# One inference step of a hybrid streaming encoder: a quarter of each weight tile's low half on GpSimd, gate1 summed on VectorE

## The chip, the core and the metric

The kernel runs on one core of a Trainium2 chip. The core has five engines with queues of their own: TensorE (PE; PEld is its weight load), VectorE (DVE), ScalarE (ACT), GpSimd (POOL) and SyncE (SP), which here issues most of the loads. The metric is the time of one execution on the device, in microseconds (us).

## What is computed

One layer of an encoder step, for 256 prompt tokens and 32 sample tokens with shared weights, D_MODEL = 2048:

```
sh1, sc1, g1, sh2, sc2, g2 = split(silu(c) @ w_mod + b_mod)      # w_mod 2048 x 12288, two rows of c
h = rms_norm(x) * (1 + sc1) + sh1
P = h @ w_in                                                     # 2048 x 14864
branch A: gated linear recurrence, 8 heads (chunkwise scan)
branch B: Mamba-2 SSD, 16 heads, convolution of width 4
branch C: chunked gMLP spatial gating
merged = sum_k sigmoid(g_k) * (y_k @ w_branch_k)
x = x + g1 * (merged @ w_out)
x = x + g2 * (relu(h2 @ w_up) ** 2 @ w_down)                     # h2 = rms_norm(x) * (1 + sc2) + sh2
y = rms_norm(x)
```

All data are float32; the states of both recurrences are outputs too.

## The kernel before

**Products.** TensorE multiplies in the type fp32r, so both factors are split into a high half (the value cast to fp32r) and a low half (what is left). Activations are split once (`hhi`/`hlo`, `yhi`/`ylo`, `mhi`/`mlo`, `h2hi`/`h2lo`, `uhi`/`ulo`). Weights are split as they arrive: `weights` (line 447) loads a tile of 128 x 4 x 256 floats (512 KB) with SyncE into one of 6 `raw` buffers, and `halves` (line 440) makes `whi` from it on ScalarE (line 443) and `wlo` on VectorE (line 444); there are 3 buffers of each. `product_group` (line 453) then does 24 matmuls per tile into two PSUM tiles: for each of 2 column blocks and 4 row blocks i, `whi` by the low activations, `whi` by the high ones and `wlo` by the high ones (lines 461 to 463). 512 tiles go this way; 56 more, of the first phase, go through `product_part` (line 418) and `halves` in the same manner.

**Order.** First phase: shift and scale of the first norm (parts 0 and 1 of w_mod) are multiplied while h is made and the first columns of `w_in` run. Then come branch C, the eight heads of branch A with their projections (`mixer_a`, line 672; until about 650 us), the sixteen of branch B (`mixer_b`), the branch products, `w_out` (about 1100 us), and from 1200 us on `w_up` and `w_down` in four slices. The recurrences take many small instructions of VectorE, ScalarE and TensorE, and some of GpSimd (memsets, copies into `att`, loads and stores of states).

**The other parts of w_mod.** They are fed in between: after each weight tile `product_group` moves a generator by a rate (`mod_rate`), and each step loads 512 KB of w_mod into a `raw` buffer (`mraw`). The order is part 2 (gate1, needed by `evac_out` from about 1100 us on), then 4, 3 and 5. Part 2 is multiplied on TensorE (lines 339 to 347): for each pair of row blocks a group of 16 entries in the trace, four column groups side by side, 32 columns wide, between other matmuls (`together`, lines 77 and 80). Parts 4, 3 and 5 are summed on VectorE (`mod_part_ve`, line 302): two multiply-adds of 128 x 512 for each of 2 row blocks of a step (line 318), one for each of the two rows of c. A unit of 512 columns ends in `mod_flush` (line 360): matmuls with ones sum over the partitions (line 375), ScalarE copies, a transpose turns (line 380), VectorE adds the bias (line 383).

**Order within an engine.** A scheduler lays the instructions of each engine into one fixed order, by the program's order and by priorities; loads and halves of weights carry a priority of 2500 places, evacuations of 1500. Each engine then runs its order strictly.

Of the kernel before, what the change touches and what calls it, by code (L numbers as in the profile page):

```python
# [10 lines left out]
F32 = mybir.dt.float32  # L11
# [3 lines left out]
ALU = mybir.AluOpType  # L15
PSUM = bass.MemoryType.PSUM

P = 128
D = 2048
NB = D // P  # L20
# [20 lines left out]
def tile_step(ctx, tc, io, outs):  # L41
    nc = tc.nc
# [8 lines left out]
    PRIO = 2500  # L51

    MOD_PARTS = (2, 4, 3, 5)
    MOD_VE = (4, 3, 5)


    MODR, RS, RA, RB, RD, RW, RC = 1.5, 0.2, 0.4, 0.3, 0.5, 0.5, 0.25

    RAW, WHI, WLO = 6, 3, 3
    MTAG = ("raw", RAW)  # L60

    MODB = 2
    EVB = 6
    BLK = 34
    TMPB = 10
# [5 lines left out]
    def nm(s):  # L71
        uid[0] += 1
        return f"{s}_{uid[0]}"

    def together(works):

        first = works[0]()  # L77
        with tc.issue_after(first.ins), tc.high_priority(offset=PRIO):
            for work in works[1:]:
                work()  # L80
# [96 lines left out]
    with tc.high_priority(offset=2 * PRIO):  # L177
        ps = aux()
# [78 lines left out]
    def par(name, j, n=1):  # L257
        i, r = off[name]
        return pcols[i][:, r + j:r + j + n]
# [42 lines left out]
    def mod_part_ve(part):  # L302


        for u in range(4):
            c0 = part * D + u * 512
            acc = [wpool.tile([P, 512], F32, tag="macc", name=nm("macc"), bufs=2) for _ in range(2)]
            for q in range(8):
                with tc.high_priority(offset=PRIO):
                    raw = wpool.tile([P, 2, 512], F32, tag=MTAG[0], name=nm("mraw"), bufs=MTAG[1])  # L310
                    nc.sync.dma_start(out=raw, in_=wm[:, 2 * q:2 * q + 2, c0:c0 + 512])
                for i in range(2):
                    for s in range(2):
                        cs = cT[:, 2 * q + i, s:s + 1]
                        if q == 0 and i == 0:
                            V.tensor_scalar_mul(out=acc[s], in0=raw[:, i], scalar1=cs)
                        else:
                            V.scalar_tensor_tensor(out=acc[s], in0=raw[:, i], scalar=cs, in1=acc[s],  # L318
                                                   op0=ALU.mult, op1=ALU.add)
                if q == 1:  # L320
                    mod_flush()
                yield
            ps = paux.tile([P, 512], F32, tag="modps", name=nm("modps"), bufs=2)
            mod_tail.append((part * NB + u * 4, 0, ps, acc))
        mod_flush()

    def mod_parts(parts):


        for part in parts:  # L330
            if part in MOD_VE:
                yield from mod_part_ve(part)
                continue
            for half in range(2):
                ps = paux.tile([P, 512], F32, tag="modps", name=nm("modps"), bufs=2)
                c0 = part * D + half * 1024
                held = []
                for k in range(NB):
                    with tc.high_priority(offset=PRIO):
                        raw = wpool.tile([P, 1024], F32, tag=MTAG[0], name=nm("mraw"), bufs=MTAG[1])  # L340
                        nc.sync.dma_start(out=raw, in_=wm[:, k, c0:c0 + 1024])
                    held.append((k, raw))
                    if len(held) == MODB:
                        together([partial(TE.matmul, ps[32 * cg:32 * cg + 32, 0:256], cT[:, k1, :],
                                          r[:, cg * 256:(cg + 1) * 256], start=k < MODB and k1 == k,
                                          stop=k == NB - 1 and k1 == held[0][0])
                                  for k1, r in reversed(held) for cg in range(4)])
                        held = []
                    if k == 1:
                        mod_flush()  # L350
                    yield
                with tc.high_priority(offset=PRIO):
                    sb = wpool.tile([P, 256], F32, tag="modsb", name=nm("modsb"), bufs=1)
                    S.copy(out=sb, in_=ps[:, 0:256])
                mod_tail.append((part * NB + half * 8, 0, ps, sb))
        mod_flush()

    mod_tail = []

    def mod_flush():  # L360

        while mod_tail:
            j, n, ps, sb = mod_tail.pop()
            if n:
                for b in range(n):
                    TE.matmul(ps[:, 2 * b:2 * b + 2], sb[:, b * P:(b + 1) * P], selm, start=True, stop=True)
                V.tensor_tensor(out=mod[:, j:j + n, :],
                                in0=ps[:, 0:2 * n].rearrange("p (b s) -> p b s", s=2),
                                in1=par("b_mod", j, n).unsqueeze(2).to_broadcast([P, n, 2]), op=ALU.add)
            else:  # L370
                nb = 2
                if type(sb) is list:
                    nb = 1
                    acc, sb = sb, wpool.tile([P, 256], F32, tag="modsb", name=nm("modsb"), bufs=1)
                    together([partial(TE.matmul, ps[32 * cg:32 * cg + 32, 0:P], ones2[:, s],
                                      acc[s][:, cg * P:(cg + 1) * P], start=s == 0, stop=s == 1)
                              for s in range(2) for cg in range(4)])
                    S.copy(out=sb[:, 0:P], in_=ps[:, 0:P])
                for b in range(nb):
                    TE.transpose(ps[:, b * P:(b + 1) * P], sb[:, b * P:(b + 1) * P], ident)  # L380
                v = ps[:, 0:nb * P].rearrange("p (b g r) -> p g b r", b=nb, r=32)
                m = mod[:, j:j + 4 * nb, :].rearrange("p (g b) s -> p g b s", b=nb)
                V.tensor_tensor(out=m, in0=v[:, :, :, 0:2], op=ALU.add,
                                in1=par("b_mod", j, 4 * nb).rearrange("p (g b) -> p g b", b=nb).unsqueeze(3)
                                .to_broadcast([P, 4, nb, 2]))


    KG = ((0, 2), (2, 2), (4, 2), (6, 2), (8, 4), (12, 4))
    boot = [(part * D + k0 * P, nk * P) for k0, nk in KG for part in (0, 1)]
    mods = chain(mod_stream(boot), mod_parts(MOD_PARTS))  # L390

    mod_count = [0]

# [43 lines left out]
                else:  # L437
                    V.tensor_add(out=acc, in0=acc, in1=pt)

    def halves(raw):  # L440
        whi = wpool.tile(list(raw.shape), F32R, tag="whi", name=nm("whi"), bufs=WHI)
        wlo = wpool.tile(list(raw.shape), F32R, tag="wlo", name=nm("wlo"), bufs=WLO)
        S.copy(out=whi, in_=raw)  # L443
        V.tensor_sub(out=wlo, in0=raw, in1=whi)  # L444
        return whi, wlo

    def weights(wv, col, q):
        with tc.high_priority(offset=PRIO):
            raw = wpool.tile([P, 4, 256], F32, tag="raw", name=nm("raw"), bufs=RAW)
            nc.sync.dma_start(out=raw, in_=wv[:, q:q + 4, col:col + 256])  # L450
            return halves(raw)

    def product_group(wv, col, nk, ahi, alo, evac, j0, n=T):
        pts = [pmain.tile([P, n], F32, tag="mm", name=nm("mm")) for _ in range(2)]
# [881 lines left out]
```

## Time and profile before

| | |
|---|---|
| median of 3 runs | 2058.45 us (2055.4 to 2059.97) |
| the profiled execution | 2054.64 us, its span 2052.9 us |
| TensorE / VectorE / ScalarE / GpSimd busy | 2002.9 / 1450.8 / 990.9 / 154.8 us |
| granted TensorE clock, mean | 0.993 |
| DMA | 412 MB, 201 GB/s on average |

Busy times count each moment once, though instructions of an engine can overlap: the next one's record begins before the last one's ends. A wait in the trace is idle time of an engine, put down to what released it. A granted clock of 1.00 is 2.4 GHz.

### The profile page before, as it was taken

The numbers are of one execution on the slowest core, as the hardware profiler recorded it, in microseconds if no ns is written. First come the engines' busy times: TensorE is split into PE (matmuls) and PEld (weight loads), VectorE is DVE, ScalarE is ACT, GpSimd is POOL, SyncE is SP. The second block draws the span as 40 slices with busy tenths as digits, with TensorE's granted clock in tenths as the row PEclk, the third lists the DMA queues.
The fourth block names the chain that finished last, engine by engine and source line by source line (L and its number), as shares of the span: only waits on it lengthen the run. The fifth ranks groups of instructions, "written<-read, shape, count | busy, mean of one in ns | idle before, by whom it ended". The sixth has DMA issues, their size and how long they took to land.

```text
span 2052.9 us, 40220 instructions
## 1 busy us (share of the span) xinstructions
PE 2002.9 (98%) x16248; PEld 1941.6 (95%) x16248; DVE 1450.8 (71%) x2515; ACT 990.9 (48%) x1547; POOL 154.8 (8%) x284
## 2 busy tenths in 40 slices
PE   5999999999999999999999999999999999999997
PEld 3888999989999999999999999999999999999997
DVE  2585767866679878798889998675864455555564
ACT  3432595675555545555344544433443344334443
POOL 3020220100101101011000100000000000000010
PEclk8999999999999999999999999999999999999999
DMA  9998745556576766577777777575655555555542
GB/s 259 312 315 267 224 137 165 176 166 200 184 226 191 212 192 199 174 229 242 226 248 235 228 237 225 185 226 185 218 192 163 162 163 166 168 165 162 167 157 88
DMA packets 364874, 412.29 MB, mean 201 GB/s; under 512 B 14808, under 2 KB 325488, under 8 KB 364688
## 3 DMA queue, kind: packets, MB, share of 16 engines
q1 hardware_dynamic: 360784, 403.97, 63.2%
q0 software_dynamic: 3040, 4.58, 1.0%
q8 instruction: 127, 2.08, 0.4%
q10 hardware_dynamic: 864, 1.18, 0.2%
q14 instruction: 59, 0.48, 0.1%
HBM read 405.05 MB, written 4.62 MB: 200 GB/s over the span
## 4 chain that ended last, share of the span: by engine, by line
PE 61%; DVE 0%; ACT 0%; DMA 0%; issue 0%; DVEq 0%; ACTq 0%
PE mm L463 20%; PE mm L461 20%; PE mm L462 20%; DMA mraw<-in_w_mod_dram 0%; PE aux L1226 0%; PE aux L210 0%; ACT stage L1300 0%; PE aux L897 0%; PE modps L77 0%; PE modps L80 0%; PE aux L80 0%; PE aux L936 0%; DVE macc L318 0%; PE aux L885 0%; DVE wlo L444 0%
## 5 line engine op out<-in xcount | busy, mean ns | idle before, releaser
L443 ACT CAST whi<-raw 128x1024 fp32r<-128x1024 f32 x568 | 595.4, 1049 | 835.9 <-PE mm L462 652.8
L444 DVE TENSOR_TENSOR wlo<-raw,whi 128x1024 fp32r<-128x1024 f32 x568 | 695.2, 1225 | 410.5 <-ACT whi L443 408.8
L461 PE MATMUL mm<-hlo,whi 128*128 128x288 f32 x1408 | 419.8, 299 | 1.2 <-ACT sg L974 1.2
L462 PE MATMUL mm<-hhi,whi 128*128 128x288 f32 x1408 | 417.1, 297 | 0.0
L463 PE MATMUL mm<-hhi,wlo 128*128 128x288 f32 x1408 | 412.3, 297 | 1.7 <-DVE wlo L444 1.7
L461 PE MATMUL mm<-h2lo,whi 128*128 128x290 f32 x1024 | 304.4, 298 | 0.0
L462 PE MATMUL mm<-h2hi,whi 128*128 128x290 f32 x1024 | 303.7, 297 | 0.0
L463 PE MATMUL mm<-uhi,wlo 128*128 128x288 f32 x1024 | 303.2, 296 | 0.0
L463 PE MATMUL mm<-h2hi,wlo 128*128 128x290 f32 x1024 | 301.8, 297 | 0.0
L462 PE MATMUL mm<-uhi,whi 128*128 128x288 f32 x1024 | 301.3, 294 | 0.0
L461 PE MATMUL mm<-ulo,whi 128*128 128x288 f32 x1024 | 301.0, 294 | 0.0
L318 DVE SCALAR_TENSOR_TENSOR macc<-mraw,cT,macc 128x512 f32<-128x512 f32 x360 | 261.3, 754 | 29.8 <-DMA mraw<-in_w_mod_dram 29.6
L461 PEld LDWEIGHTS mm<-hlo,whi 128*128 128x128 f32 x1408 | 265.5, 189 | 4.7 <-issue 2.2
L463 PEld LDWEIGHTS mm<-hhi,wlo 128*128 128x128 f32 x1408 | 263.2, 189 | 3.7 <-DVE wlo L444 2.6
L462 PEld LDWEIGHTS mm<-hhi,whi 128*128 128x128 f32 x1408 | 265.9, 189 | 0.5
L463 PEld LDWEIGHTS mm<-h2hi,wlo 128*128 128x128 f32 x1024 | 194.3, 190 | 0.3 <-issue 0.2
L462 PEld LDWEIGHTS mm<-h2hi,whi 128*128 128x128 f32 x1024 | 194.5, 190 | 0.0
L461 PEld LDWEIGHTS mm<-h2lo,whi 128*128 128x128 f32 x1024 | 193.6, 189 | 0.5 <-issue 0.4
L461 PEld LDWEIGHTS mm<-ulo,whi 128*128 128x128 f32 x1024 | 193.0, 188 | 0.4 <-issue 0.4
L462 PEld LDWEIGHTS mm<-uhi,whi 128*128 128x128 f32 x1024 | 192.4, 188 | 0.0
L463 PEld LDWEIGHTS mm<-uhi,wlo 128*128 128x128 f32 x1024 | 192.2, 188 | 0.1
L430 PE MATMUL mm<-hlo,whi 128*128 128x288 f32 x448 | 136.8, 306 | 0.4 <-DVE hlo L530 0.4
(421 smaller groups left out, 3079.8 us busy)
## 6 DMA issues: line engine op xcount, KB each, us to landing
raw<-in_w_in_dram SPq DMA_DIRECT2D x204, 512.0 KB, 4.4
mraw<-in_w_mod_dram SPq DMA_DIRECT2D x128, 512.0 KB, 4.3
raw<-in_w_up_dram SPq DMA_DIRECT2D x128, 512.0 KB, 3.8
raw<-in_w_down_dram SPq DMA_DIRECT2D x128, 512.0 KB, 3.5
raw<-in_w_mod_dram SPq DMA_DIRECT2D x64, 512.0 KB, 5.9
raw<-in_w_branch_dram SPq DMA_DIRECT2D x48, 512.0 KB, 4.5
raw<-in_w_out_dram SPq DMA_DIRECT2D x32, 512.0 KB, 4.7
raw<-in_w_in_dram SPq DMA_DIRECT2D x56, 256.0 KB, 5.1
```

Of the source, the lines that this page charges most:

```text
L318: V.scalar_tensor_tensor(out=acc[s], in0=raw[:, i], scalar=cs, in1=acc[s], op0=ALU.mult, op1=ALU.add)
L430: TE.matmul(pt, whi[:, i, cs], alo[k], start=i == 0, stop=False)
L443: S.copy(out=whi, in_=raw)
L444: V.tensor_sub(out=wlo, in0=raw, in1=whi)
L461: TE.matmul(pts[b], whi[:, i, cs], alo[k], start=k == 0, stop=False)
L462: TE.matmul(pts[b], whi[:, i, cs], ahi[k], start=False, stop=False)
L463: TE.matmul(pts[b], wlo[:, i, cs], ahi[k], start=False, stop=k == nk - 1)
```

## The change

`halves` gets a flag. For the 512 tiles of `weights`, VectorE subtracts only the first three of the tile's four row blocks (768 of 1024 columns), and GpSimd the fourth. The 56 tiles of the first phase stay whole on VectorE. And part 2 of w_mod goes the way of the other three, `mod_part_ve`; the function for TensorE goes.

```
     def halves(raw, shared=False):
...
         S.copy(out=whi, in_=raw)
-        V.tensor_sub(out=wlo, in0=raw, in1=whi)
+        n = 3 if shared else raw.shape[1]
+        V.tensor_sub(out=wlo[:, 0:n], in0=raw[:, 0:n], in1=whi[:, 0:n])
+        if shared:
+            G.tensor_sub(out=wlo[:, 3], in0=raw[:, 3], in1=whi[:, 3])
         return whi, wlo

     def weights(wv, col, q):
...
-            return halves(raw)
+            return halves(raw, True)

-    def mod_parts(parts):
...
-                    if len(held) == MODB:
-                        together([partial(TE.matmul, ps[32 * cg:32 * cg + 32, 0:256], cT[:, k1, :],
-                                          r[:, cg * 256:(cg + 1) * 256], start=k < MODB and k1 == k,
-                                          stop=k == NB - 1 and k1 == held[0][0])
-                                  for k1, r in reversed(held) for cg in range(4)])
...
-    mods = chain(mod_stream(boot), mod_parts(MOD_PARTS))
+    mods = chain(mod_stream(boot), *[mod_part_ve(part) for part in MOD_PARTS])
```

The rest of the diff is `mod_flush`, whose branch for part 2's two tails goes; the sums and the transpose of a VectorE unit stay as they were.

The order on VectorE, before, near the 103rd low half, while a head of branch A ends (`stA` are its states, `pad` a copy for it):

```order
L444 TENSOR_TENSOR wlo_5793<-raw_5790,whi_5792 128x1024
L444 TENSOR_TENSOR wlo_5823<-raw_5820,whi_5822 128x1024
L600 COPY pad_106<-aux_5409 32x128
L444 TENSOR_TENSOR wlo_5892<-raw_5889,whi_5891 128x1024
L700 COPY stA_5421<-aux_5417 128x128
L701 SCALAR_TENSOR_TENSOR stA_5422<-stA_5421,eb_5399,aux_5417 128x128
L703 SCALAR_TENSOR_TENSOR stA_5423<-sA_5415,eb_5399,aux_5417 128x128
```

And now, at the 103rd low half (L405 is the subtract, L315 part 2's multiply-add, L663 to L666 are the states):

```order
L405 TENSOR_TENSOR wlo_5864<-raw_5861,whi_5863 128x768
L663 COPY stA_5300<-aux_5296 128x128
L315 SCALAR_TENSOR_TENSOR macc_5561<-mraw_5923,cT,macc_5561 128x512
L315 SCALAR_TENSOR_TENSOR macc_5562<-mraw_5923,cT,macc_5562 128x512
L664 SCALAR_TENSOR_TENSOR stA_5301<-stA_5300,eb_5278,aux_5296 128x128
L666 SCALAR_TENSOR_TENSOR stA_5302<-sA_5294,eb_5278,aux_5296 128x128
L315 SCALAR_TENSOR_TENSOR macc_5561<-mraw_5923,cT,macc_5561 128x512
L405 TENSOR_TENSOR wlo_5895<-raw_5892,whi_5894 128x768
L315 SCALAR_TENSOR_TENSOR macc_5562<-mraw_5923,cT,macc_5562 128x512
```

Part 2's multiply-adds, 128 in all, now lie between the subtracts from the 30th to the 138th low half; 39 of them between the 100th and the 120th.

The order on GpSimd, before, around a head of branch A (`atc` and `att` are its scores, `sA` and `stA` states that go in and out):

```order
L664 COPY att_5098<-atc_5099 32x32
L676 MEMSET atc_5272 128x96
L695 DMA sA_5415<-in_state_hgrn_dram 128x128
L705 DMA out_dram<-stA_5249 128x128
```

And now, around a head's end (L407 is the quarter):

```order
L625 COPY att_5323<-atc_5324 32x2x32 x4
L627 COPY att_5323<-atc_5324 32x32
L407 TENSOR_TENSOR wlo_6216<-raw_6213,whi_6215 128x256
L407 TENSOR_TENSOR wlo_6259<-raw_6256,whi_6258 128x256
L639 MEMSET atc_6394 128x96
L658 DMA sA_6537<-in_state_hgrn_dram 128x128
L668 DMA out_dram<-stA_5474 128x128
L669 DMA out_dram<-stA_5475 128x128
L407 TENSOR_TENSOR wlo_6290<-raw_6287,whi_6289 128x256
```

GpSimd had one queue of the recurrences' own work; now 512 quarters, each of which TensorE's matmuls of row block 3 wait for, stand between it.

## Rows read from the trace of the kernel before

**Rows 1.** The page's busy times: us, share of the span, instructions.
```profile
PE 2002.9 (98%) x16248; PEld 1941.6 (95%) x16248; DVE 1450.8 (71%) x2515; ACT 990.9 (48%) x1547; POOL 154.8 (8%) x284
```
**Rows 2.** Waits: engine, line, tile <- releaser: us in total, times, longest.
```profile
ACT whi L443 <- PE mm L462: 652.8, 364, 3.6
...
PE aux L77 <- DVE z L632: 2.9, 1, 2.9
...
PE mm L463 <- DVE wlo L444: 1.7, 2, 1.1
```
**Rows 3.** Busy us by stretch: length, PE, PEld, DVE, ACT, POOL (xcount), clock, DMA.
```profile
200.00:600.00 400.00, 391.27 (x3688) 372.21 (x3687) 285.31 (x612) 254.15 (x404) 51.46 (x98) 0.99 0.61 185
457.00:532.00 75.00, 73.82 (x797) 69.77 (x796) 47.69 (x103) 42.50 (x68) 6.91 (x17) 1.00 0.65 196
600.00:1000.00 400.00, 396.42 (x3298) 389.96 (x3298) 350.45 (x628) 219.79 (x355) 47.26 (x91) 1.00 0.68 208
1000.00:1200.00 200.00, 200.00 (x1553) 197.81 (x1552) 183.72 (x300) 88.09 (x140) 13.93 (x11) 1.00 0.75 234
1100.00:1200.00 100.00, 100.00 (x776) 98.53 (x775) 97.36 (x176) 47.73 (x85) 13.93 (x11) 1.00 0.73 228
```
**Rows 4.** Timeline of PE around one group (start, us), and all its matmuls on L80.
```profile
404.40 0.29 PE L462 MATMUL mm<-hhi,whi 128*128 128x288 f32 x1
404.54 0.29 PE L463 MATMUL mm<-hhi,wlo 128*128 128x288 f32 x1
...
405.76 0.51 PE L724 MATMUL aux<-sq,ones 128*128 128x288 f32 x1
...
L80 PE MATMUL modps<-mraw,cT x224: 379/379/404, 206.0 to 585.9; 128*32 128x256 f32 x112
```
**Rows 5.** Timeline of PE around the tail of a VectorE unit.
```profile
874.44 0.30 PE L463 MATMUL mm<-yhi,wlo 128*128 128x288 f32 x1
...
875.24 0.40 PE L461 MATMUL mm<-hlo,whi 128*128 128x288 f32 x1
```
**Rows 6.** Groups: xcount | busy us, mean ns | idle before <- releaser.
```profile
L444 DVE TENSOR_TENSOR wlo<-raw,whi 128x1024 fp32r<-128x1024 f32 x568 | 695.2, 1225 | 410.5 <-ACT whi L443 408.8
...
L318 DVE SCALAR_TENSOR_TENSOR macc<-mraw,cT,macc 128x512 f32<-128x512 f32 x360 | 261.3, 754 | 29.8 <-DMA mraw<-in_w_mod_dram 29.6
...
L1249 DVE TENSOR_TENSOR ulo<-r,uhi 128x288 fp32r<-128x288 f32 x64 | 28.7, 452 | 0.1
```
**Rows 7.** Timeline of DVE and POOL from 961 to 964 us.
```profile
961.13 0.75 DVE L318 SCALAR_TENSOR_TENSOR macc<-mraw,cT,macc 128x512 f32<-128x512 f32 x1
...
961.79 1.22 DVE L444 TENSOR_TENSOR wlo<-raw,whi 128x1024 fp32r<-128x1024 f32 x1
...
962.93 1.31 DVE L318 SCALAR_TENSOR_TENSOR macc<-mraw,cT,macc 128x512 f32<-128x512 f32 x1
...
961.94 1.74 POOL L949 TENSOR_TENSOR ssB<-ssB,sq 128x288 f32<-128x288 f32 x1 [16.63 <-ACT sq L944]
```
**Rows 8.** Timeline of POOL and DVE at 227 us.
```profile
227.22 0.82 POOL L1031 TENSOR_TENSOR sumC<-sumC,acc 128x288 f32<-128x288 f32 x1 [0.32 <-ACT acc L1026]
...
227.21 0.45 DVE L438 TENSOR_TENSOR acc<-acc,mm 128x288 f32<-128x288 f32 x1 [0.61 <-PE mm L432]
```
**Rows 9.** DVE's subtracts (L444) alone by the stretches of rows 3: length, busy (xcount).
```profile
200.00:600.00 400.00, 124.02 (x101) 0.99 0.61 185
457.00:532.00 75.00, 24.31 (x20) 1.00 0.65 196
600.00:1000.00 400.00, 136.81 (x112) 1.00 0.68 208
1000.00:1200.00 200.00, 73.08 (x60) 1.00 0.75 234
1100.00:1200.00 100.00, 35.33 (x30) 1.00 0.73 228
```
**Rows 10.** A group of DMA issues on POOL.
```profile
L202 POOL DMA_DIRECT2D xs<-in_x_sample_dram x16 | 8.8, 559 | 0.4 <-issue 0.4
```

More of the change, by code (lines that the diff above doesn't have):

```diff
@@ L53, in tile_step @@
     MOD_PARTS = (2, 4, 3, 5)
-    MOD_VE = (4, 3, 5)
     MODR, RS, RA, RB, RD, RW, RC = 1.5, 0.2, 0.4, 0.3, 0.5, 0.5, 0.25
@@ L60, in tile_step @@
     MTAG = ("raw", RAW)
-    MODB = 2
     EVB = 6
@@ L325, in mod_part_ve @@
         mod_flush()
-    def mod_parts(parts):
[L330 to L342, printed above, removed]
-                    if len(held) == MODB:
-                        together([partial(TE.matmul, ps[32 * cg:32 * cg + 32, 0:256], cT[:, k1, :],
-                                          r[:, cg * 256:(cg + 1) * 256], start=k < MODB and k1 == k,
-                                          stop=k == NB - 1 and k1 == held[0][0])
-                                  for k1, r in reversed(held) for cg in range(4)])
[L348 to L356, printed above, removed]
     mod_tail = []
@@ L370, in mod_flush @@
             else:
[L371 to L385, printed above, removed]
+                sums, sb = sb, wpool.tile([P, P], F32, tag="modsb", name=nm("modsb"), bufs=1, padded_shape=[P, 512])
+                together([partial(TE.matmul, ps[32 * cg:32 * cg + 32, 0:P], ones2[:, s],
+                                  sums[s][:, cg * P:(cg + 1) * P], start=s == 0, stop=s == 1)
+                          for s in range(2) for cg in range(4)])
+                S.copy(out=sb, in_=ps[:, 0:P])
+                TE.transpose(ps[:, 0:P], sb, ident)
+                V.tensor_tensor(out=mod[:, j:j + 4, :], in0=ps[:, 0:P].rearrange("p (g r) -> p g r", r=32)[:, :, 0:2],
+                                in1=par("b_mod", j, 4).unsqueeze(2).to_broadcast([P, 4, 2]), op=ALU.add)
     KG = ((0, 2), (2, 2), (4, 2), (6, 2), (8, 4), (12, 4))
     boot = [(part * D + k0 * P, nk * P) for k0, nk in KG for part in (0, 1)]
-    mods = chain(mod_stream(boot), mod_parts(MOD_PARTS))
+    mods = chain(mod_stream(boot), *[mod_part_ve(part) for part in MOD_PARTS])
     mod_count = [0]
@@ L438, in product_part, with halves @@
                     V.tensor_add(out=acc, in0=acc, in1=pt)
-    def halves(raw):
+    def halves(raw, shared=False):
         whi = wpool.tile(list(raw.shape), F32R, tag="whi", name=nm("whi"), bufs=WHI)
```

## The prediction

> **What bounds the kernel now.** First the page's busy times: TensorE is busy for 98% of the span, VectorE (DVE) for 71%, GpSimd (POOL) for 8% [rows 1]. Then the list of waits, because a busy share says nothing of who waits for whom: TensorE's matmuls waited for a low half (`wlo`) twice in the whole span, 1.7 us together, while ScalarE waited 364 times, 652.8 us, for TensorE to give back a buffer of high halves [rows 2]. So the weights are always ready ahead of TensorE, by up to the three buffers of `whi` and `wlo`, and a shorter DVE instruction is worth nothing by itself: only matmul work that goes away shortens the span, and only as long as nobody else becomes late. Last the busy time by stretches, for DVE's reserve: 285.3 of 400 us from 200 to 600 us, 350.5 of 400 to 1000, 183.7 of 200 to 1200, and in the last 100 us of that 97.36 while TensorE was still at 100.00 [rows 3]. The last row is the yardstick: DVE may be 97% busy and still hold nobody up.
>
> **The change part by part.**
>
> *Matmuls of part 2 (gate1) go.* In the trace one of them is a group of 16: the last matmul before it starts at 404.54, the next after it at 405.76, against 0.14 between neighbours without a group [rows 4]. That is 1.22 - 0.14 = 1.08 us, and the 224 matmuls of line 80, 14 of each group, make 16 groups between 206 and 586 us [rows 4]: 17.3 us of TensorE time. All of it lies on the path, since TensorE is the bound.
>
> *Four tails come instead of two.* A tail of the DVE kind holds TensorE from 874.44 to 875.24, 0.80 - 0.14 = 0.66 us [rows 5], and a transpose of at most 0.14 after it: 0.8 us, four times, 3.2 us; the two tails that go had two transposes each and no sums, some 0.5 us together. Net on TensorE: -17.3 + 3.2 - 0.5 = **-14.6 us**.
>
> *128 multiply-adds come to DVE.* They are the kind that takes 754 ns on average [rows 6]; back to back one starts 0.66 us after the other (961.13 and 961.79) [rows 7]. In the new order they stand between the 30th and the 138th low half, so nearly all in the stretch from 200 to 600 us: 120 x 0.66 = 79 us there. 39 of them stand between the 100th and the 120th low half, which were made from 457 to 532 us.
>
> *DVE's subtract shrinks to 768 columns.* 1024 columns take 1225 ns, 288 take 452 [rows 6]: 1.05 ns a column, so 768 take 0.96 us and each tile saves 0.27 us. 512 of the 568 tiles are shared (138 us over the span). ScalarE's cast and the loads stay as they are; part 2's 32 loads of 512 KB stay 32 loads of the same size, in rows half as long.
>
> *The quarter goes to POOL.* No row has a 128x256 subtract there. A 128x288 addition takes 0.82 us beside a DVE instruction that reads PSUM [rows 8], so the quarter is between 0.73 (by its columns) and 0.82 us. 512 of them are 400 us of an engine with 1900 us free, beside TensorE's 3.2 us per tile.
>
> *What the quarter does to DVE.* This is the open price. At 961.94 POOL's addition of two SBUF tiles waits behind DVE's subtract (until 963.01) and ends 0.67 us after it; the DVE multiply-add that follows takes 1.31 us, not 0.75 [rows 7]. So DVE lost 0.56 us to one POOL instruction of 288 columns, 0.50 for 256. Where the next DVE instruction takes an operand from PSUM it lost nothing: 0.45 us at 227.21, as without POOL [rows 8]. The Trainium skill says it as a rule ("SBUF — State Buffer", section "Who interferes with whom"): a DVE instruction with two SBUF inputs and a GpSimd instruction that reads SBUF exclude each other, and the later one blocks fully until the first is done. The trace agrees, with 0.56 us lost where the rule at its worst would take the whole 0.82; by that worst the change comes out as rival C at its upper end.
>
> Per tile DVE therefore changes by -0.27 us (POOL never in the way) up to -0.27 + 0.56 = +0.29 us (always). By the order about 65% of DVE's instructions read two SBUF tiles; 0.65 x 0.50 - 0.27 = **+0.06 us**, which I take: the quarter does not relieve DVE at all, it roughly pays for itself.
>
> *Is DVE still below its limit?* From 200 to 600 us 82 of the 101 tiles [rows 9] are shared: 285.3 + 79 + 82 x 0.06 = 369 us, with bounds 342 and 388, in a stretch that now lasts 400 - 14.6 = 385 us. That is 96%, just under the yardstick. The tight place is 457 to 532 us: 47.7 [rows 3] + 39 x 0.66 + 20 x 0.06 = 74.6 us (bounds 68 and 79) in 72 us (75 without its share, a fifth, of the groups that go). The two tiles, 6 us, that lie ready ahead of TensorE could hide the overhang of 2.6 us, but it will not come evenly: I count 3 us (bounds 0 and 8). From 1100 to 1200 us there are 97.4 + 30 x 0.06 = 99 us (89 to 106) of 100: 1 us (0 to 6). From 600 to 1000 even the upper bound is 350.5 + 112 x 0.29 = 383 of 400.
>
> *Waits for the recurrences.* TensorE runs in order and waited once 2.9 us for a DVE product of the A mixer [rows 2]. With DVE fuller these products come later, but the new order also puts their matmuls later, by up to 200 of the main matmuls. I take +3 us (bounds -5 and +8).
>
> *POOL's queue.* It runs in order, and behind memsets, state transfers and copies into `att` the next quarter waits. A DMA issue holds POOL 0.56 us [rows 10]. The usual bunch is three of them and a memset, 2 us, less than the lead of two tiles; the longest, ten issues (5.6 us) near 965 us, about equals it. 0 us (up to 3).
>
> **The sum.** -14.6 + 3 + 1 + 3 = -7.6 us. The profiled execution took 2054.64 us, of it 2052.9 in the span: 2047.0. It lies 3.8 us below the median of the runs shown (2058.45, from 2055.4 to 2059.97), so the forecast in terms of that median is **2051 us**, -0.4%. A measurement of this kernel can tell 0.2% (4 us) from no change.
>
> **The rivals.**
> - *A, the forecast* (0.35): DVE stays just under full, TensorE keeps half of what it won; 2045 to 2053.
> - *D, all of it* (0.15): POOL finds gaps or runs beside DVE instructions that read PSUM; DVE is relieved by up to 0.27 us per tile, nobody is late, and the later place of the A mixer's matmuls saves a few of the old waits. -14.6 - 3: 2041. For it: DVE sat idle 408.8 us before its subtracts, waiting for ScalarE's cast [rows 6], so there are gaps; against it that most of them lie after 1200 us, where DVE is not needed.
> - *B, nothing to see* (0.18): the overhang of the tight places adds up to 10 to 15 us at the bounds above, or POOL's queue holds a quarter up now and then; 2055 to 2062. That is also the case in which the change does not do what it says: DVE has as much to do as before.
> - *C, slower* (0.32): one mechanism, DVE blocked behind the quarter, on two sides of its limit. Its place is every shared tile up to 1200 us. It decides once a quarter costs DVE more than 0.53 us on average: then 82 x 0.26 = 21 us fill the stretch to 600 us (364 without any such cost, of 385). At a block of 0.67 us on every tile (net +0.40) DVE needs 397 of 385 us there, 208 of 200 from 1000 to 1200, and with the tight places' 15: +12 + 8 + 7 - 14.6, about 2071 in terms of the median. At the whole 0.82 (net +0.55) it needs 409 of 385, 412 of 400 and 217 of 200: +24 + 12 + 17 - 14.6 = +38, 2097. For it speaks that `raw` and `whi` are two SBUF tiles on both engines and that both are released by the same cast; against it that the measured loss was 0.56 and often nothing.
>
> **How the numbers follow.** The likeliest case gives 2051 us; its own range is 2045 to 2053. The range of 8 in 10 reaches from D with its waits saved, 2037, into the lower half of C, 2083; above it about 0.15 is left out, below it 0.03. Faster by over 0.2% are A and D, 0.50; within 0.2% is B, 0.18; slower is C, 0.32.
>
> **What would show it.** Right: TensorE's instructions lose the 128 wide `modps<-mraw` matmuls and its busy time falls by 13 to 16 us; DVE's multiply-adds rise from 360 to 480 with a mean above 754 ns, and its busy time rises by about 120 us (bounds -45 and 240); the subtract of 768 columns has a mean well above 0.96 us, and POOL's quarter one above 0.82, because they block each other; TensorE's waits for `wlo` stay below 10 us. D: the 768-column subtract at 0.96 us. C: DVE at 97% or more from 200 to 600 and from 600 to 1200 us, TensorE waiting for `wlo` (DVE's three quarters or POOL's one) for tens of us, and a granted clock below 0.99 there. The forecast is wrong if TensorE's busy time does not fall, or if POOL's queue rather than DVE is what it waits for.

## The result and the profile after

The change makes the kernel **slower: 2123.82 us** (median of 4 runs, 2121.04 to 2125.63) against 2059.21 us (2055.4 to 2062.64; one run more than in the table ahead), a ratio of 1.031 [1.030, 1.033]. The forecast was 2051 us, 2037 to 2083, faster. The direction was wrong, and the time lies beyond the upper end of the range.

The page's busy times of the changed kernel, to be held against [rows 1]:

```profile
PE 2014.6 (95%) x16056; PEld 1952.1 (92%) x16056; DVE 1512.1 (71%) x2645; ACT 1009.5 (48%) x1561; POOL 787.8 (37%) x796
```

TensorE (PE) has 192 instructions fewer: the 256 entries of part 2's wide matmuls are gone, as foreseen, and 64 of the tails' sums came. Yet it is 11.7 us busier, and it stands idle for 2123.9 - 2014.6 = 109.3 us instead of 50.0. VectorE (DVE) is 71% busy, as before. Of the waits (engine, line, tile <- releaser: us in total, times, longest) these matter; in the numbering of this kernel L403 is ScalarE's cast, L405 DVE's three quarters, L407 POOL's quarter, L424 to L426 are the matmuls, and L413 is the issue of a weight tile's load on SyncE:

```profile
PE mm L426 <- DVE wlo L405: 24.6, 27, 3.2
...
PE aux L74 <- DVE mpad L892: 9.4, 4, 5.7
...
PE mm L424 <- ACT whi L403: 6.7, 2, 4.9
PE aux L1027 <- DVE yC L1032: 5.4, 2, 3.8
...
ACT whi L403 <- PE mm L425: 456.5, 234, 5.8
ACT whi L403 <- POOL wlo L407: 72.8, 39, 2.5
...
SPq L413 <- POOL wlo L407: 135.6, 233, 1.1
```

Where TensorE waited twice for a low half [rows 2], it now waits 27 times (and twice in the first phase, 1.3 us), and each time for DVE: nowhere in the list of its waits is POOL's quarter. Over the whole list, TensorE's waits that DVE ended come to 55.1 us, against 8.7 before: 25.9 for low halves (1.7 before) and 29.2 for DVE's other products, above all of the recurrences and of branch C (7.0 before). Those that ScalarE ended rose from 11.9 to 22.4. ScalarE's cast, which before waited for TensorE to give a buffer back and for loads, now also waits 39 times until POOL gives a buffer of high halves back, and the loads wait 233 times until POOL gives back `raw`. The stretches (length, PE, PEld, DVE, ACT, POOL busy, clock, DMA), beside [rows 3]:

```profile
200.00:600.00 400.00, 367.25 (x3304) 353.97 (x3303) 347.44 (x705) 237.12 (x381) 126.44 (x163) 0.96 0.57 173
457.00:532.00 75.00, 70.01 (x663) 67.30 (x663) 73.68 (x149) 40.75 (x64) 24.48 (x38) 0.98 0.66 195
600.00:1000.00 400.00, 373.08 (x3047) 361.83 (x3045) 319.72 (x582) 224.89 (x349) 151.27 (x192) 0.99 0.62 186
1000.00:1200.00 200.00, 199.31 (x1549) 196.71 (x1548) 185.53 (x278) 89.45 (x131) 78.36 (x75) 1.00 0.76 235
1200.00:1600.00 400.00, 391.42 (x2943) 387.41 (x2943) 303.49 (x455) 171.49 (x267) 159.53 (x128) 1.00 0.65 206
```

From 200 to 600 us DVE is 87% busy and TensorE idle for 33 us; from 600 to 1000 us DVE is *less* busy than before (320 against 350 of 400) and TensorE idle for 27 us. So DVE does not run out of time on the whole; single instructions come late. The time is lost in pieces of at most 5.7 us from 200 to 1450 us, and nothing after that (TensorE idle for 10.9 us, before 11.1).

The groups (xcount | busy us, mean ns | idle before), beside [rows 6]:

```profile
L407 POOL TENSOR_TENSOR wlo<-raw,whi 128x256 fp32r<-128x256 f32 x512 | 650.9, 1272 | 1004.3 <-ACT whi L403 961.3 <-PE mm L425 7.3 <-DVE sg L944 4.5
L405 DVE TENSOR_TENSOR wlo<-raw,whi 128x768 fp32r<-128x768 f32 x512 | 506.6, 993 | 341.7 <-ACT whi L403 337.5 <-PE aux L687 2.9
L315 DVE SCALAR_TENSOR_TENSOR macc<-mraw,cT,macc 128x512 f32<-128x512 f32 x480 | 392.2, 852 | 61.5 <-DMA mraw<-in_w_mod_dram 60.6
```

DVE's subtract takes 0.99 us, near the 0.96 of the estimate; the quarter takes 1.27 us, not 0.73 to 0.82, and the multiply-adds 852 ns, not 754. The timelines of DVE and of POOL show how that comes:

```profile
622.69 0.95 DVE L405 TENSOR_TENSOR wlo<-raw,whi 128x768 fp32r<-128x768 f32 x1
623.56 1.88 DVE L315 SCALAR_TENSOR_TENSOR macc<-mraw,cT,macc 128x512 f32<-128x512 f32 x2
...
622.70 1.53 POOL L407 TENSOR_TENSOR wlo<-raw,whi 128x256 fp32r<-128x256 f32 x1 [1.27 <-ACT whi L403]
```

Both begin when the cast is done, DVE runs first, POOL ends 0.59 us after it, and the two multiply-adds behind take 1.88 us where two back to back take 0.66 + 0.75 = 1.41 [rows 7]. It is the mutual block of [rows 7] again; below it is called the lock. So it goes for 253 of the 512 quarters: they start together with DVE's subtract and end between 0.59 and 0.60 us after it (the middle eight tenths of them).

One long stall, of ScalarE and then of TensorE (timelines of the changed kernel):

```profile
968.34 0.42 ACT L889 ACTIVATE m<-m 128x256 f32<-128x256 f32 x1 [3.26 <-DVE m L886]
968.78 1.28 ACT L937 ACT_TABLE_LOAD   x1
970.07 0.41 ACT L937 ACTIVATE sg<-mm 128x288 f32<-128x288 f32 x1
970.50 1.28 ACT L888 ACT_TABLE_LOAD   x1
...
973.04 1.28 ACT L937 ACT_TABLE_LOAD   x1
974.34 0.41 ACT L937 ACTIVATE sg<-mm 128x288 f32<-128x288 f32 x1
974.76 1.28 ACT L889 ACT_TABLE_LOAD   x1
...
976.82 0.25 ACT L891 ACTIVATE mpad<-mpad 32x64 f32<-32x64 f32 x1
...
971.53 0.29 PE L424 MATMUL mm<-ylo,whi 128*128 128x288 f32 x1
977.47 0.29 PE L74 MATMUL aux<-mpad,xdt 128*64 128x32 f32 x1 [5.65 <-DVE mpad L892]
...
981.92 0.44 PE L425 MATMUL mm<-hhi,whi 128*128 128x288 f32 x1
982.16 0.43 PE L426 MATMUL mm<-hhi,wlo 128*128 128x288 f32 x1
...
982.95 0.30 PE L425 MATMUL mm<-hhi,whi 128*128 128x288 f32 x1
983.08 0.29 PE L426 MATMUL mm<-hhi,wlo 128*128 128x288 f32 x1
```

In the new order two gates (`sg`, sigmoid) stand between the exponentials of a head of branch B. Each change between the two makes ScalarE load a table, 1.28 us; `mpad` comes late and TensorE waits 5.65 us. And that is not all: its clock was granted at half for a stretch that begins in the stall, as the windows say (columns as above):

```profile
960.00:971.00 11.00, 10.83 (x82) 10.61 (x81) 7.45 (x14) 5.61 (x9) 3.49 (x5) 1.00 0.72 226
...
975.61:982.43 6.82, 4.96 (x28) 4.66 (x29) 4.87 (x10) 3.16 (x6) 1.50 (x1) 0.50 0.48 139
```

At 1.2 GHz matmuls start 0.24 us apart (981.92, 982.16), at 2.4 GHz 0.13 (982.95, 983.08).

Over the span the mean granted clock fell from 0.993 to 0.984. By the clock in the trace, TensorE was busy at half the clock for 46.8 us, before for 14.2; half of such time is lost, so this costs 23.4 - 7.1 = 16.3 us. With 59.3 us more idle time and the 14.6 us that went, this makes +61 of the 71 us between the two profiled spans; the other 10 lie in a busy time that I can't split further.

### The profile page after: what moved, and what is told of

Same layout as the page of the kernel before. It is cut to its first block, busy times and chain, and to the rows that moved or that the text cites. A ratio compares the mean times of both kernels' runs of the same rounds, so it can differ in the third digit from the quotient of the medians.

```text
span 2123.9 us, 41480 instructions
## 1 busy us (share of the span) xinstructions
PE 2014.6 (95%) x16056; PEld 1952.1 (92%) x16056; DVE 1512.1 (71%) x2645; ACT 1009.5 (48%) x1561; POOL 787.8 (37%) x796
## 5 line engine op out<-in xcount | busy, mean ns | idle before, releaser
L407 POOL TENSOR_TENSOR wlo<-raw,whi 128x256 fp32r<-128x256 f32 x512 | 650.9, 1272 | 1004.3 <-ACT whi L403 961.3
L403 ACT CAST whi<-raw 128x1024 fp32r<-128x1024 f32 x568 | 594.4, 1048 | 783.9 <-PE mm L425 456.5
L405 DVE TENSOR_TENSOR wlo<-raw,whi 128x768 fp32r<-128x768 f32 (+1 forms) x568 | 576.0, 1017 | 389.8 <-ACT whi L403 385.4
L315 DVE SCALAR_TENSOR_TENSOR macc<-mraw,cT,macc 128x512 f32<-128x512 f32 x480 | 392.2, 852 | 61.5 <-DMA mraw<-in_w_mod_dram 60.6
L426 PE MATMUL mm<-hhi,wlo 128*128 128x288 f32 x1408 | 421.5, 303 | 14.3 <-DVE wlo L405 14.1
L424 PE MATMUL mm<-hlo,whi 128*128 128x288 f32 x1408 | 424.0, 302 | 7.6 <-ACT whi L403 6.7
L425 PE MATMUL mm<-hhi,whi 128*128 128x288 f32 x1408 | 423.0, 301 | 0.0
L426 PE MATMUL mm<-uhi,wlo 128*128 128x288 f32 x1024 | 304.0, 297 | 2.3 <-DVE wlo L405 2.3
L424 PE MATMUL mm<-h2lo,whi 128*128 128x290 f32 x1024 | 305.6, 298 | 0.0
L426 PE MATMUL mm<-h2hi,wlo 128*128 128x290 f32 x1024 | 304.0, 297 | 0.0
L424 PE MATMUL mm<-ulo,whi 128*128 128x288 f32 x1024 | 302.8, 296 | 0.0
L426 PEld LDWEIGHTS mm<-hhi,wlo 128*128 128x128 f32 x1408 | 269.1, 192 | 19.1 <-DVE wlo L405 18.1
L424 PEld LDWEIGHTS mm<-hlo,whi 128*128 128x128 f32 x1408 | 270.5, 192 | 9.9 <-ACT whi L403 7.2
L425 PEld LDWEIGHTS mm<-hhi,whi 128*128 128x128 f32 x1408 | 270.8, 192 | 0.4
L426 PEld LDWEIGHTS mm<-uhi,wlo 128*128 128x128 f32 x1024 | 193.1, 189 | 2.8 <-DVE wlo L405 2.8
L426 PEld LDWEIGHTS mm<-h2hi,wlo 128*128 128x128 f32 x1024 | 195.4, 191 | 0.2 <-DVE wlo L405 0.2
L424 PEld LDWEIGHTS mm<-ulo,whi 128*128 128x128 f32 x1024 | 193.9, 189 | 0.5 <-issue 0.4
L424 PEld LDWEIGHTS mm<-h2lo,whi 128*128 128x128 f32 x1024 | 193.8, 189 | 0.3 <-issue 0.2
```

The costliest lines, as they stand in the source:

```text
L405: V.tensor_sub(out=wlo[:, 0:n], in0=raw[:, 0:n], in1=whi[:, 0:n])
L407: G.tensor_sub(out=wlo[:, 3], in0=raw[:, 3], in1=whi[:, 3])
L424: TE.matmul(pts[b], whi[:, i, cs], alo[k], start=k == 0, stop=False)
L425: TE.matmul(pts[b], whi[:, i, cs], ahi[k], start=False, stop=False)
L426: TE.matmul(pts[b], wlo[:, i, cs], ahi[k], start=False, stop=k == nk - 1)
```

## The experiments

All times in us; "idle" is the profiled span less TensorE's busy time; "tables" are ScalarE's table loads. Each ratio is to the kernel before as timed beside that run (medians 2057.7 for runs 1 to 4, 2059.2 for 5 to 8, 2059.8 for 9 to 11, 2059.6 for 12). Busy time, idle time and clock are those of one profiled execution; the mean clock of executions of one kernel differs by up to 0.006 (0.985 to 0.991 in run 3), so smaller differences in that column say nothing.

| kernel | median | ratio to before | PE busy | idle | clock | tables |
|---|---|---|---|---|---|---|
| before (with the change) | 2059.2 | | 2002.9 | 50.0 | 0.993 | 82 |
| the change | 2123.8 | 1.031 | 2014.6 | 109.3 | 0.984 | 94 |
| 1 part 2 alone | 2065.8 | 1.0038 [1.0023, 1.0053] | 1998.3 | 66.4 | 0.988 | 91 |
| 2 quarter alone | 2103.7 | 1.0222 [1.0206, 1.0238] | 2020.7 | 82.4 | 0.988 | 94 |
| 3 quarter as memsets | 2072.0 | 1.0066 [1.0043, 1.0090] | 2000.7 | 73.8 | 0.985 | 94 |
| 4 quarter of a constant | 2104.1 | 1.0222 [1.0198, 1.0247] | 2012.8 | 90.1 | 0.983 | 94 |
| 5 before, no tables | 2046.7 | 0.9936 [0.9918, 0.9955] | 1998.4 | 46.7 | 0.994 | 6 |
| 6 the change, no tables | 2091.4 | 1.0154 [1.0135, 1.0172] | 2003.3 | 86.3 | 0.989 | 6 |
| 7 part 2, no tables | 2049.5 | 0.9951 [0.9934, 0.9968] | 1990.0 | 55.4 | 0.991 | 6 |
| 8 memsets, no tables | 2047.1 | 0.9938 [0.9918, 0.9958] | 1989.9 | 57.0 | 0.996 | 6 |
| 9 part 2 spread | 2055.9 | 0.9979 [0.9970, 0.9988] | 1993.6 | 61.2 | 0.995 | 82 |
| 10 half of part 2, no tables | 2039.8 | 0.9902 [0.9887, 0.9917] | 1990.6 | 48.7 | 0.992 | 6 |
| 11 constant, no tables | 2076.4 | 1.0079 [1.0065, 1.0093] | 2003.5 | 71.5 | 0.987 | 6 |
| 12 part 2 spread more | 2047.3 | 0.9949 [0.9934, 0.9964] | 1989.1 | 56.8 | 0.992 | 76 |

### 1. Part 2 alone

To the kernel before:

```
-    MOD_VE = (4, 3, 5)
+    MOD_VE = (2, 4, 3, 5)
```

> The kernel before with part 2 summed on DVE and no quarter on GpSimd. Four theories stand for the +65 us of the change. Lock: a quarter on POOL and a two-SBUF instruction of DVE hold each other up, so both come late. Hold: POOL returns raw and whi late (ScalarE's cast waited 72.8 us for POOL in the changed kernel), lock or not. Part 2: the 128 multiply-adds fill DVE from 200 to 600 us, the quarter is harmless. Order: the new order of ScalarE and DVE (94 table loads on ScalarE instead of 82) is what makes the recurrences late. Lock and Hold expect 2045 to 2057 us (TensorE loses 14.6 us, the tight place from 457 to 532 us takes up to 10 back), with no wait of ScalarE's cast for POOL. Part 2 expects 2095 to 2125. Order expects something between, 2060 to 2100, since the order here is new too.

Measured: 2065.8 us, +8. Only the interval of the order theory holds that. TensorE's waits and ScalarE's timeline in this kernel (L443 is the cast, L461 the matmul that needs it):

```profile
PE mm L461 <- ACT whi L443: 7.3, 5, 4.9
```

```profile
283.31 1.28 ACT L813 ACT_TABLE_LOAD   x1
284.60 0.44 ACT L813 ACTIVATE ldt<-ldt 16x288 f32<-16x288 f32 x1
285.06 1.28 ACT L814 ACT_TABLE_LOAD   x1
286.35 0.44 ACT L814 ACTIVATE ldt<-ldt 16x288 f32<-16x288 f32 x1
286.70 1.03 ACT L443 CAST whi<-raw 128x1024 fp32r<-128x1024 f32 x1
```

The wait of 4.9 us is for the cast at 286.70, which stands behind table loads. So even without POOL TensorE did not keep its 14.6 us: it is 16.4 us more idle, and in this execution another 6.9 us go to the half clock while it works (14.0 against 7.1).

### 2. The quarter alone

To the kernel before: the new `halves` and its call, with part 2 left on TensorE.

> The kernel before with the quarter on GpSimd alone; part 2 stays on TensorE. Lock and Hold expect most of the loss without the 14.6 us won: 2100 to 2140 us, with the cast waiting tens of us for POOL and TensorE idle some 50 us or more between 200 and 1450 us. Part 2 expects 2055 to 2065, as before. Order expects 2070 to 2110.

Measured: 2103.7 us, +46. Lock and hold stand, and so does the loss foreseen by the order theory; part 2 as the cause of the whole falls. The cast waits 70.8 us for POOL, as foreseen; TensorE is idle for 44 us from 200 to 1600 us, a little less than foreseen, and here 3.2 us of its waits, one wait, are for POOL's quarter. The stretches:

```profile
200.00:600.00 400.00, 390.81 (x3673) 370.75 (x3672) 276.64 (x607) 258.81 (x407) 155.00 (x179) 0.99 0.58 183
...
600.00:1000.00 400.00, 375.58 (x3065) 364.15 (x3065) 322.99 (x592) 218.92 (x345) 153.99 (x192) 0.99 0.60 186
```

From 200 to 600 us, with DVE 69% busy, the same quarters cost nothing (TensorE 390.8, before 391.3 [rows 3]). They cost 20 us from 600 to 1000, where DVE is 81% busy.

### 3 and 4. The quarter without a read, and with a read of something else

To the changed kernel, in `halves`; first run 3, then run 4 (`sh_c` is a constant tile of zeros):

```
-            G.tensor_sub(out=wlo[:, 3], in0=raw[:, 3], in1=whi[:, 3])
+            for _ in range(2):
+                G.memset(wlo[:, 3].bitcast(F32), 0.0)
```

```
-            G.tensor_sub(out=wlo[:, 3], in0=raw[:, 3], in1=whi[:, 3])
+            G.tensor_sub(out=wlo[:, 3], in0=sh_c, in1=sh_c)
```

> The changed kernel with POOL's quarter replaced by two memsets of the same columns: POOL writes wlo but reads nothing from SBUF, and neither raw nor whi waits for it. The order on DVE, ScalarE and SyncE is the changed kernel's almost row for row. Left out: the low half of every fourth row block of the weights. Lock and Hold expect 2035 to 2055 us: DVE's 768-column subtract at 0.96 us on average, multiply-adds of part 2 back near 0.75, no cast waiting for POOL. Part 2 expects 2095 to 2125 still, less at most 10 for DVE's shorter subtract. Order expects 2090 or more, as the order is the same.

> The changed kernel with POOL's quarter as a subtraction of a constant tile from itself: POOL reads two operands from SBUF as before, so a lock against DVE stays, but raw and whi no longer wait for POOL. Left out: the low half of every fourth row block of the weights. Lock expects 2095 to 2125 us, as in the change, with POOL's quarter at 1.2 us on average and DVE's two-SBUF instructions lengthened by about 0.5. Hold expects 2035 to 2060, the cast no longer waiting for POOL. Part 2 and Order expect 2095 to 2125.

Measured: 2072.0 and 2104.1 us. Run 3 lies in none of the intervals: 17 us above that of lock and hold, 13 or more below the others. Run 4 lies in that of the lock and in those of part 2 and the order, and far above that of the hold alone. The groups of run 3:

```profile
L405 DVE TENSOR_TENSOR wlo<-raw,whi 128x768 fp32r<-128x768 f32 x512 | 490.4, 960 | 389.8 <-ACT whi L403 350.9 <-issue 20.5 <-POOL att L639 8.7
L315 DVE SCALAR_TENSOR_TENSOR macc<-mraw,cT,macc 128x512 f32<-128x512 f32 x480 | 344.8, 755 | 62.9 <-DMA mraw<-in_w_mod_dram 62.2
L408 POOL MEMSET wlo<- 128x256 f32 x1024 | 320.6, 313 | 1290.7 <-PE mm L427 1255.4 <-PE mm L391 3.8 <-issue 2.8
```

and of run 4:

```profile
L408 DVE TENSOR_TENSOR wlo<-raw,whi 128x768 fp32r<-128x768 f32 x512 | 500.7, 981 | 358.8 <-ACT whi L406 320.8 <-issue 13.5 <-POOL wlo L410 9.0
L410 POOL TENSOR_TENSOR wlo<-shc 128x256 fp32r<-128x256 f32 x512 | 417.1, 815 | 1210.2 <-PE mm L429 900.4 <-issue 155.8 <-DVE macc L315 42.6
L315 DVE SCALAR_TENSOR_TENSOR macc<-mraw,cT,macc 128x512 f32<-128x512 f32 x480 | 378.6, 823 | 59.4 <-DMA mraw<-in_w_mod_dram 58.7
```

While POOL only writes, DVE's instructions have their undisturbed lengths (960 and 755 ns). Once it reads SBUF, they grow, and the kernel loses 32 us: **the lock**. From run 4 to the change it loses another 20: there `raw` and `whi` wait for POOL, and the quarter starts together with DVE's own subtract (its mean goes from 815 to 1272 ns). Which of these two does more is open; I call both **the hold**. What neither explains is left in run 3: 6 us more than run 1, though each of 512 subtracts is 0.27 us shorter there.

How the low halves come late can be counted. I pair the k-th subtract of DVE with the k-th tile's first matmul on `wlo`, 568 pairs. From 200 to 1600 us, those finished less than 0.3 us ahead of their matmul are 3 before, 9 in run 1, 11 in run 3, 35 in run 4 and 45 in the change. In the stretch from 200 to 600 us the median time from the end of the cast to DVE's subtract is 0.03 us before and in run 2, 1.23 in run 1, 1.50 in run 3, 1.84 in run 4, 2.55 in the change: part 2's multiply-adds stand in front of the subtract, and the lock makes the wait longer. The count is not the time, though: run 9 below has 18 such low halves, twice as many as run 1, and is 10 us faster. POOL's quarter, paired the same way with the first matmul of row block 3, is never less than 0.77 us ahead in the change.

### 5 to 8. Without table loads

To the kernel before (5), the change (6), run 1 (7) and run 3 (8); the order of all other instructions stays row for row. A line of some 32 alike:

```
-        S.activation(out=xbc[j][:, 0:SEQ], in_=cv[:, 0:SEQ], func=AF.Silu)
+        S.activation(out=xbc[j][:, 0:SEQ], in_=cv[:, 0:SEQ], func=AF.Abs)
```

> The kernel before with every Silu, Gelu, Sigmoid, Exp, Ln and Sqrt on ScalarE (but three in the setup) put in as Abs: the order on every engine stays as it is, but ScalarE has 6 table loads of 1.28 us instead of 82. The activations are no longer the reference's. Two theories for the part of the loss that neither lock nor hold explains (8 us with part 2 alone, 6 more with a quarter that reads nothing): Tables: the new order mixes activation functions at places where TensorE waits for ScalarE, the stall costs its own length and then a stretch at 1.2 GHz. Fullness: VectorE is simply too full for the recurrences from 200 to 600 us. For this run both expect little, 2045 to 2057 us, since ScalarE was late for TensorE by only a few us before; it is the base for the next three.

> The changed kernel with the same replacement (94 table loads become 6; the activations are not the reference's). Lock and hold are untouched. Tables expects the stalls for mpad near 977 us (5.7 us), for whi near 286 us (4.9), and for modsb and iv near 630 us to go, with their stretches at 1.2 GHz: 2085 to 2105 us. Fullness expects 2112 to 2122.

> Part 2 on VectorE alone, no quarter, with the same replacement (91 table loads become 6; the activations are not the reference's). Tables expects the stalls of 4.9, 3.7, 1.2 and 1.2 us that wait for ScalarE to go, with two or three stretches at 1.2 GHz: 2042 to 2050 us, below the kernel before in the same form by 5 to 12 us, as the 14.6 us of TensorE's time then come through. Fullness expects 2055 to 2064, no better than the kernel before in the same form.

> The changed kernel with the memsets in place of the quarter (no lock, no hold; the low half of every fourth row block left out) and the same replacement of the activations. Tables expects the 4.5 us stall for mpad near 942 us and the 4.9 us one near 286 to go: 2038 to 2048 us, as fast as part 2 alone in the same form or up to 5 us faster. Fullness expects 2060 to 2070.

Measured: 2046.7, 2091.4, 2049.5 and 2047.1 us. Runs 5, 6 and 8 fall where the theory of the tables had them. ScalarE's busy time falls by 97.0 us from before to run 5, and 76 loads of 1.283 us are 97.5: the rest of ScalarE's work took as long as before. Without its table loads the change is 32.4 us faster, the kernel before 12.4: so **20 us of the loss hang on table loads**. The stall of 5.65 us for `mpad` is gone in run 6 (the longest wait for it is 1.1), and TensorE no longer waits for the cast. Run 3's remainder over run 1 is gone (8 against 7: -2.4, with runs that overlap). Run 7 splits the theories: it is in the interval of the tables, but not below run 5 as they foresaw; it is 2.8 us above. Of ScalarE's stalls that were to go, the one of 3.7 us (for `iv`, line 604) is still there, so no table load made it. TensorE's 14.6 us are still given back. The stretch to 600 us, in run 5:

```profile
200.00:600.00 400.00, 395.48 (x3743) 376.81 (x3743) 290.69 (x629) 207.51 (x377) 50.96 (x98) 1.00 0.60 188
```

and in run 7:

```profile
200.00:600.00 400.00, 385.20 (x3529) 373.34 (x3528) 362.29 (x741) 204.59 (x371) 53.83 (x98) 0.99 0.61 187
```

With DVE at 362 instead of 291 us, TensorE idles 10 us more there. That fits the theory of fullness, for part 2 alone; runs 9, 10 and 12 try it.

### 9. Part 2 spread

To run 1:

```
-    MODR, RS, RA, RB, RD, RW, RC = 1.5, 0.2, 0.4, 0.3, 0.5, 0.5, 0.25
+    MODR, RS, RA, RB, RD, RW, RC = 1.5, 0.2, 0.3, 0.35, 0.5, 0.5, 0.25
```

> Part 2 on VectorE, no quarter, and the steps of w_mod fed more evenly: 0.3 a weight tile during branch A instead of 0.4, 0.35 instead of 0.3 during branch B. With 0.4 part 2 alone took 2065.8 us. Density (VectorE is locally too full where part 2's multiply-adds stand): some 26 us of VectorE's work leave the stretch from 200 to 600 us, TensorE's stalls of 2.7 and 3.7 us near 403 and 508 shrink, 2046 to 2058 us, perhaps faster than the kernel before. Order (it is chance which evacuation or table load the new order puts in the way): anything from 2050 to 2070, with the table loads that this order has (82 instead of 91) on the good side. No effect of the spread: 2062 to 2069.

Measured: 2055.9 us, in the interval of density: 10 us faster than run 1, and 0.2% faster than the kernel before. That lies in the interval of the order too. The stall of 4.9 us at 288 us is still there; those of 2.7 and 3.7 us are gone. From 200 to 600 us there are 113 multiply-adds instead of 128, and at most 31 instead of 41 between 20 low halves; but DVE's busy time in that stretch did not fall (349.4 us, in run 1 348.7): other work moved up as TensorE went faster (384.6 us busy, in run 1 375.0). The density of the multiply-adds and the number of tables both fell (91 to 82), so the run does not part them.

### 10. Half of part 2, no tables

To run 7, in the loop over the rows `s` of c in `mod_part_ve`:

```
                     for s in range(2):
+                        if part == 2 and s and (q or i):
+                            continue
```

> Part 2 on VectorE alone with Abs in place of the activations (2049.5 us so far), and of part 2 only the multiply-adds of the first row of c, 68 instead of 128 (gate1 of the second row left out). Fullness of VectorE expects that TensorE now keeps most of the 14.6 us it won: 2036 to 2043 us. If the stalls come from where the order puts single instructions, and not from VectorE's load, it stays at 2045 to 2052.

Measured: 2039.8 us. With 60 multiply-adds fewer on DVE the kernel is 9.7 us faster than run 7 and 6.9 faster than run 5, and idle time is back at 48.7 us. That is what DVE's load as the cause foresaw, and the stretch below agrees. It is not shown alone, since the order moved with it: some tenth of the other instructions stand elsewhere (206 of 2133 on DVE, 144 of 1467 on ScalarE), not much less than between the kernel before and run 1 (250 and 202).

```profile
200.00:600.00 400.00, 393.26 (x3611) 383.40 (x3610) 336.76 (x708) 210.99 (x383) 51.73 (x98) 0.99 0.63 192
```

### 11. The lock alone, no tables

To run 4, the replacement of runs 5 to 8.

> The changed kernel with Abs in place of the activations, and POOL's quarter as a subtraction of a constant tile from itself: the lock without the hold of raw and whi (the low half of every fourth row block left out). The changed kernel in this form took 2091.4 us, with memsets 2047.1. With the activations as they are the lock cost 32 us (2104.1 against 2072.0) and the hold 20 (2123.8 against 2104.1). If these add up independently of the table loads: 2070 to 2080 us. If the lock is what turns late table loads into stalls: 2050 to 2062, and the hold is the larger part. If the lock is all: 2085 to 2092.

Measured: 2076.4 us: the lock costs 2076.4 - 2047.1 = 29 us, the hold 2091.4 - 2076.4 = 15. With tables they are 32 and 20, about the same.

### 12. Part 2 spread more

To run 1, with rates whose order has few table loads (76) and no long work between two casts near 288 us:

```
-    MODR, RS, RA, RB, RD, RW, RC = 1.5, 0.2, 0.4, 0.3, 0.5, 0.5, 0.25
+    MODR, RS, RA, RB, RD, RW, RC = 1.5, 0.1, 0.25, 0.4, 0.5, 0.5, 0.25
```

> As the run with part 2 spread, but 0.1 of a w_mod step a weight tile before branch A, 0.25 during it and 0.4 during branch B (that run, with 0.2, 0.3 and 0.35, took 2055.9 us, of it 4.9 us in one stall at 288 us for a cast that stood behind three table loads, and a stretch at 1.2 GHz after it). In this order ScalarE has 76 table loads instead of 82, and nowhere between two casts in that region more than 6.2 us of other work by the listed lengths, where it was 8.3. If density and the place of the table loads are what kept TensorE's 14.6 us from coming through: 2045 to 2052 us, the stall at 288 us gone. If not: 2053 to 2060, as the work moved into branch B (85 instead of 80 multiply-adds there in the fullest 40 tiles) makes new stalls.

Measured: **2047.3 us, 0.5% faster than the kernel before** (0.9949 [0.9934, 0.9964]). TensorE waits for ScalarE's cast near 288 us for 1.1 us, not 4.9. Its page and the stretch:

```profile
PE 1989.1 (97%) x16056; PEld 1936.4 (95%) x16056; DVE 1526.7 (75%) x2645; ACT 986.0 (48%) x1543; POOL 159.7 (8%) x284
```

```profile
200.00:600.00 400.00, 388.14 (x3552) 376.80 (x3551) 341.74 (x722) 249.46 (x413) 50.46 (x98) 1.00 0.56 174
```

TensorE's busy time is 13.8 us below that of before, as forecast for part 2; idle time takes 6.8 back between these two executions, and by the medians 12.3 us come through. Of the change, one half (part 2 on DVE) is worth keeping, with other rates; the other (the quarter) is not. Whether the kernel before would gain from these rates as well, with part 2 left on TensorE, was not run.

## Why the prediction was wrong

- **TensorE's net 14.6 us: right in size, but the sign named for it failed.** Busy time was to fall by 13 to 16 us and rose by 11.7, which the prediction named as a sign of being wrong. In run 12, whose clock is that of before, it is 13.8 us lower; against run 5, in the same form without tables, it is 8.4 lower in run 7 and 7.8 in run 10. Taking off half of the busy time that lay at half the clock on either side, the fall is 14.7 in run 12, 13.0 in run 7, 10.9 in run 10 and 4.6 in the change: there the clock hides 16.3 us, and the other 10 stay open.
- **128 multiply-adds, subtract of 0.96 us: right.** 480 multiply-adds, 960 ns undisturbed, 993 in the change; the sign "well above 0.96" did not come.
- **The price of the lock for DVE: too high, if anything.** Taken were 0.65 x 0.50 = 0.33 us a quarter, net +0.06. From run 3 to the change DVE's busy time rises from 1402.9 to 1512.1 us: 109 / 512 = 0.21, net -0.06; so its busy time rose by 61 us from before, where 120 were forecast. The Trainium skill's rule ("SBUF — State Buffer", section "Who interferes with whom") that a DVE instruction with two SBUF inputs contends with a GpSimd instruction that reads SBUF, and not with one that only writes it, agrees with runs 3 and 4 (755 against 823 ns).
- **"Is DVE still below its limit?": the step that failed.** I summed DVE's busy time, found 96%, and held it against a yardstick from 1100 to 1200 us, where DVE at 97% held nobody up. That stretch is `w_out`: subtracts, multiply-adds and evacuations in a steady row. Counted over the same weight tiles, the places that I priced as tight stayed near my bounds: in the change TensorE is idle for 6.4 us in the 19 tiles that ran from about 457 to 532 us (3, bounds 0 and 8) and for 6.0 in the 30 from 1100 to 1200 (1, bounds 0 and 6); before, for nothing. Most of the loss lies where the sum left room: 31 us idle in the rest of the tiles from 200 to 600 us (before 9) and 22 in those from 600 to 1000 (before 4), where even my upper bound stayed below the limit. There the recurrences run, and lateness is decided by single instructions, not by the sum. In the change DVE has 13% to spare to 600 us and 20% to 1000 us, and from 200 to 1600 us 45 low halves come at the last moment. "The two tiles, 6 us, that lie ready ahead of TensorE could hide the overhang" fell with it: to 600 us the median low half was 4.8 us ahead of its matmul before and 2.6 in the change, and a tenth of them were 0.06 us or less ahead (before 3.0). I gave these two places 3 + 1 us; TensorE's waits for low halves rose by 24.2 us, and the lock alone, by medians, is 29 to 32.
- **"Waits for the recurrences", +3 us: mis-sized.** TensorE's waits for DVE's other products rose by 22.2 us (7.0 to 29.2), far beyond the bound of 8. Some of it hangs on table loads, as for `mpad` (0.7 before, 9.4 in the change, 1.9 in run 6 without its table loads).
- **"ScalarE's cast and the loads stay as they are": false.** I counted a quarter as an instruction of POOL's queue and not as one more reader that holds `raw` and `whi`. The cast waits 72.8 us for POOL; the hold is 15 to 20 us. That POOL's own queue would not be what TensorE waits for was right, even with quarters of 1.27 us.
- **Nothing in the sum for ScalarE's order and for the clock.** I read the new order on DVE and POOL alone. On ScalarE it has 94 table loads instead of 82, some of them in front of what TensorE needs: 20 us of the loss goes with the tables. And stalls are paid again in the clock: 16.3 us over the span, part of all the sums above.
- **Rival C** had the sign and, with the lock, one of the mechanisms; and two of its signs came: TensorE waited 24.6 us for DVE's three quarters, and the clock was 0.96 from 200 to 600 us. But it decided by DVE being full, at 97% or more; DVE was 87% and 80% busy. Its 2097 us had no term for the hold, the tables and the clock.
- **The range.** Its lower end, 2037, comes out of no sum: with the bound of -5 for the waits, D is 2039. The upper end, 2083, lies within C; the time came above even C's worst, 2097.

The loss in steps, by medians: part 2 alone +8, the quarter's new order without a read +6 (run 3 less run 1), the lock +32, the hold +20: 66 of 65 us. The lock, the hold and the share of the tables are shown by runs that change one thing in an order that stays the same or almost so. Without table loads the first two steps together are +0.4 us (run 8 less run 5), not +14, so nearly all of these 14 us go with the tables. Why the forecast gain of 14.6 us does not come through even there, by DVE's load or by the order, stays open.

## What to carry to other kernels

A share of busy time taken from a stretch of steady bulk work is no yardstick for one with recurrences: there count how far ahead the operands are, and what lengthens single instructions. An instruction moved to GpSimd holds the buffers that it reads for longer and, if it reads SBUF, lengthens those of VectorE that read two SBUF tiles (755 to 823 ns here); ask first whether the engine that it relieves is waited for at all (here relief without a price, run 8 against run 7, was worth 2.4 us, too little to tell from none). And where a change makes a scheduler lay the program anew, read the order of every engine, table loads on ScalarE above all: a few rates of the feeding (run 12 against run 1) were worth 18 us, in which density and table loads are not parted.

## What the runs showed of the hardware

- 76 table loads of ScalarE, 1.28 us each, cost this kernel, bound by TensorE, 12.4 us (run 5 against before), though ScalarE was 48% busy. The Trainium skill ("ScalarE: Activation LUTs", section "Table sets: the hidden batching unit") says to batch activations by table set. No run here does that; runs 5 to 8 show what the loads cost.
- A stall of TensorE can cost more than its length. Beginning within the 5.65 us above, the granted clock was 0.50 for 6.8 us, of which TensorE worked 4.96: about 2.5 us more for the work done in them.
- GpSimd's subtract of 128x256 takes between 0.71 and 3.49 us in the change, half of them 1.51 or more. When it starts together with DVE's subtract of 0.96 us (253 times), it takes 1.51 us and ends 0.6 us after it; else its median is 0.88. A memset of the same columns takes 0.31 us and leaves DVE's lengths alone (960 and 755 ns in run 3).
